# The input stage of a pool and RG-LRU decoder layer: order by a list scheduler in place of an order by hand

## The chip, the cores and the metric

The kernel runs on one core of a Trainium2 chip. The metric is device time in microseconds (us), the median of several executions; lower is better. The core has five engines that each work through their own list of instructions in order and meet at semaphores: TensorE (PE in the profile; its weight loads are PEld), VectorE (DVE), ScalarE (ACT), GpSimd (POOL) and SyncE (SP), which here issues every DMA.

## The reference

One layer of a decoder, in float32, over 2048 prompt tokens and 8 sequences of 8 new tokens (2112 tokens together, 1024 channels):

```
xn = rms_norm(x, norm_pre)
z  = xn @ w_in                                  # 1024 -> 4096: pool input V | gate G | lru input U | gate L
pool: causal means of V over windows 2/4/8/16 minus the token, one 256x256 map a group, a scale a channel
lru:  causal conv of width 4 on U -> r, i = sigmoid(block-diagonal maps)
      a = exp(-8 r softplus(-lam));  h = a h + sqrt(max(1 - a^2, 1e-12)) * i * u      # scan over time
out = concat(pool * silu(G), lru * silu(L)) @ w_out                                   # 2048 -> 1024
y   = x + rms_norm(out, norm_post)
```

The new states of the pool, the conv and the LRU are returned too.

## The kernel before, in words

Channels lie on the partitions and tokens along the free axis. Each float32 operand of a matrix product is split into a high and a low half of a reduced type (`split`, lines 123 to 131: a copy on ScalarE makes the high half, a subtraction makes the low one), and each product is three matmuls (high by high, high by low, low by high).

**Input stage.** The tokens are cut into three passes m of 704 (`MW`), each into two chunks of 352 columns. In a pass, the 32 blocks of 128 output channels are taken in 16 quads of two blocks: kind V, G, U or L, and p from 0 to 3. The list `QUADS` holds them in order. In pass 0 a quad is eight products of 12 matmuls (`plain_slot`). In passes 1 and 2 it is seven (a Strassen-like scheme, `quad_slot`, order 1, 5, 6, 3, 7, 2, 4 in `ORDER`); products 1, 6, 7 and 4 use one PSUM bank in turn (names a1V, a2G and so on in the profile), 5 and 3 a second (e), 2 a third (d). After each product the bank is emptied, by a copy on ScalarE (`put_copy`, L878) or a sum on VectorE (`put_sum`, L874), before the next product may use it. The seven combinations of x that the products multiply (X11, T1, T2, X22, T3, X21, T4) are made once for a pass, in the stretch called a transition, during the last quad of one pass and the first of the next. Those of the weights are made during passes 0 and 1, split, stored to DRAM (`wsd`), and loaded into half tiles (tag w, `W_BUFS` buffers of them) seven slots ahead of use (`w_step`).

Each finished quad starts a chain of work on the other engines: `silu_chain` for the gates, `pool_chain` (window sums, split, map, multiplication by the gate, store), and for the LRU `conv_chain`, then `lru_chain` (gates, exp, tanh, sqrt, a scan on VectorE, multiplication by the gate, store). `x_chain` prepares the tokens of the next pass. The chains keep their intermediate values in tiles of tag t (`T_BUFS`) and e (`E_BUFS`).

**What sets the order.** The stage is written under a manual schedule, so each engine runs its instructions as they are emitted. `one_slot` emits one product on TensorE, then the evacuations of the product before, then due DMAs, then pieces of chains. Each chain is a generator that yields what its next piece costs VectorE, ScalarE and GpSimd, in us, and how many slots to wait:

```
yield 0, 1.8, 0, 0        # lru_chain, after exp and tanh
return evac, {3: 0.5, 7: 0.5, 2: 0.5}.get(pid, 0.0)      # quad_slot: what an evacuation costs VectorE
```

`run_gens` goes on taking pieces while the slot's budget of 1.92 us (`SLOT`) an engine lasts. When a producer on another engine is done is not known to it; the number of slots to wait stands for that. What a transition emits in which slot is a table by hand (`plan` in `transition`). Stores go through `later`, which issues them two slots on.

**Output stage.** Eight pairs of token tiles, seven products each, with 512 columns a matmul. The first five first products (`p1`) are emitted inside the manual schedule, as 15 slots; the rest is ordered by the framework. Weights sit in regions 0, 1 and 2 of the old x storage; `combos_chain` makes the combinations of `w_out` during pass 2 and stores them (`wtd`), `region_chain` and `t3_chain` load and split them.

Of the kernel before, what the change touches and what calls it, by code (L numbers as in the profile page):

```python
# [55 lines left out]
SLOT = 1.92  # L56
# [7 lines left out]
def hymba_kernel(  # L64
# [656 lines left out]
    dmas, pe_q, gens = [], [], []  # L721
    now = [0]

    def later(slots, fn):
        dmas.append((now[0] + slots, fn))

    def due_dmas(force=False):
        for item in list(dmas):
            if force or item[0] <= now[0]:
                dmas.remove(item)  # L730
                item[1]()
# [3 lines left out]
    IDLE = [XN[:, BASE[n] + 1024 * i:BASE[n] + 1024 * (i + 1)] for n in ("X11", "T2", "T1") for i in range(2)]  # L735

# [7 lines left out]
    def store_w(flat, kind, p, pid, slots=2):  # L744
        key = (KINDS[kind] // 8 * NG + p) * 7 + pid - 1
        later(slots, lambda: nc.sync.dma_start(out=wsd[:, key, :], in_=flat.bitcast(F32)))

    def flat_of(t):
        return t.rearrange("p a b -> p (a b)")

    def plain_tile(q, n):
        t = w_tiles[q, n] = half_tile(f"w{q[2]}{q[1]}_{n}")
        split(t[:, 0, :], t[:, 1, :], w_rawt[q, n], AC, V)
        if n in PLAIN_PID:
            store_w(flat_of(t), q[2], q[1], PLAIN_PID[n])
        return 0.65, 0.62, 0.0

    n_idle = [0]

    def s_sums(q, i):  # L760
# [10 lines left out]
    S_OF = {5: "22", 6: "11", 7: "21", 3: "12"}  # L771

    def s_prep(q, i):
        if q[2] not in EARLY:
            return 0.0, 0.0, 0.0
        s_sums(q, i)
        dve, act = 0.65, 0.0
        for pid in ((), (5,), (6, 7), (3,))[i]:
            b = IDLE[n_idle[0] % len(IDLE)]
            n_idle[0] += 1  # L780
            split(b[:, :512], b[:, 512:], w_rawt[q, S_OF[pid]], AC, V)
            store_w(b, q[2], q[1], pid)
            dve, act = dve + 0.65, act + 0.62
        return dve, act, 0.0

    def w_step(q, i):
        m, p, kind = q
        pid = ORDER[i]
        t = w_tiles[q, pid] = half_tile(f"w{m}{kind}{p}_{pid}")
        if not is_late(q) or pid in (1, 2, 4):  # L790
            key = (KINDS[kind] // 8 * NG + p) * 7 + pid - 1
            nc.sync.dma_start(out=flat_of(t).bitcast(F32), in_=wsd[:, key, :])
        if not is_late(q) or i > 4:
            return 0.0, 0.0, 0.0
        if i < 4:
            s_sums(q, i)
        if not i:
            return 0.65, 0.0, 0.0
        split(t[:, 0, :], t[:, 1, :], w_rawt[q, S_OF[pid]], AC, V)
        store_w(flat_of(t), kind, p, pid)  # L800
        return 1.3 if i < 4 else 0.65, 0.62, 0.0
# [3 lines left out]
    def load_small(m, kind, p):  # L805
# [77 lines left out]
    def plain_slot(q, i):  # L883
        t = Q[q]
        j, h, c = PLAIN[i]
        n = f"{j + 1}{h + 1}"
        w = w_tiles[q, n]
# [5 lines left out]
        def evac():  # L893
            if h:
                put_copy(q, j, c, z)
            if i == 7:
                quad_end(q)
        return evac, 0.0

    def quad_slot(q, i):  # L900
# [3 lines left out]
        pid = ORDER[i]  # L904
        w = w_tiles.pop((q, pid))
# [4 lines left out]
        z = t[key]  # L910
        quad_product(z, w, XOF[pid], first, True, True)

        def evac():
            if pid == 1:
                put_copy(q, 0, 0, z)
            elif pid == 5:
                put_copy(q, 1, 1, z)
            elif pid == 6:
                put_copy(q, 0, 1, z)
            elif pid == 3:  # L920
                put_sum(q, 0, 1, z)
            elif pid == 7:
                put_sum(q, 1, 1, z)
            elif pid == 2:
                put_sum(q, 0, 0, z)
            else:
                put_copy(q, 1, 0, z)
                quad_end(q)
        return evac, {3: 0.5, 7: 0.5, 2: 0.5}.get(pid, 0.0)

    def spawn(gen, delay=1, need=0, rank=2):
        gens.append([gen, now[0] + delay, need, rank])
        gens.sort(key=lambda g: g[3])

    def quad_end(q):
        if q[2] in "GL":
            spawn(silu_chain(q), need=1)
        else:
            for g in {"V": lambda: [pool_chain(q)], "U": lambda: [conv_chain(q, j) for j in range(2)]}[q[2]]():
                spawn(g)  # L940

    def silu_chain(q):
        for j in range(2):
            g = Q[q]["dst"][j][:, :MW]
            AC.activation(out=g, in_=g, func=AF.Silu)
            yield 0, 0.85, 0, 0
# [7 lines left out]
    def pool_chain(q):  # L954
# [3 lines left out]
        c = L / 1000.0 * 1.05 + 0.1  # L958
        ds = []
        for j, blk in enumerate(blocks("V", p)):  # L960
            E = Q[q]["dst"][j]
            if m < LM:
                G.tensor_copy(out=hp[:, blk, :], in_=E[:, MW:MW + PB])
            else:
# [3 lines left out]
                later(3, lambda blk=blk, op=op: nc.sync.dma_start(out=o_pool[blk], in_=op))  # L968
            S, sh = E, 1
            while sh < w:  # L970
                while e_free() < 1:
                    yield 0, 0, 0, 1
# [5 lines left out]
                yield c, 0, 0.4 if sh == 1 else 0, 0  # L978
                S, sh = dst, 2 * sh
            if m == 0:  # L980
# [13 lines left out]
            yield c, 0, 0, 1  # L994
        Q[q]["d"] = []
        prev = Q.get((m, p - 1, "V") if p else (m - 1, NG - 1, "V"))
        while prev and not prev.get("maps"):
            yield 0, 0, 0, 1
        while t_free() < 1:
            yield 0, 0, 0, 1  # L1000
        load_small(m, "pw", p)
        for j, d in enumerate(ds):
            dh = e_tile(f"dh{m}_{p}{j}", F32R)[:, :MW]
            AC.copy(out=dh, in_=d)  # L1004
            yield 0, 0.8, 0, 1
            while e_free() < 1:
                yield 0, 0, 0, 1
# [4 lines left out]
            yield 0, 0, 1.8, 0  # L1012
        sums.add((m, p))
        yield 0, 0, 0, 3
        while not Q.get((m, p, "G"), {}).get("silu"):
            yield 0, 0, 0, 1
        for c in range(2):
            for j in range(2):
                pe_q.append((now[0] + 1, lambda j=j, c=c: pool_map(q, j, c)))

    def pool_map(q, j, c):
        m, p, _ = q
        pw = small["pw"]
# [6 lines left out]

# [3 lines left out]
        def evac():  # L1034
            assert Q[m, p, "G"].get("silu")
            V.scalar_tensor_tensor(out=g[:, cs], in0=Y, scalar=col(C_SCALE, blk), in1=g[:, cs],
                                   op0=ALU.mult, op1=ALU.mult)
            if c == 1:
# [3 lines left out]
                def store():  # L1042
                    nc.sync.dma_start(out=mixed[:, blk, m * MW:(m + 1) * MW], in_=g[:, :MW])
                    t_done(1)
                later(2, store)
        return evac, 0.55

    def conv_chain(q, j):
# [4 lines left out]
        while prev and not prev.get("gates"):  # L1053
            yield 0, 0, 0, 1
        while t_free() < (3 if j or m else 4):
            yield 0, 0, 0, 1
# [3 lines left out]
        E = Q[q]["dst"][j]  # L1060
        xs = t_chain(f"xs{b}_{m}")[:, :n]
# [8 lines left out]
        yield 0, 0.9, 0.4, 1  # L1070
        for k in range(CB):
            V.scalar_tensor_tensor(out=xs, in0=E[:, k:k + n], scalar=col(C_CW + 8 * k, b), in1=xs,  # L1072
                                   op0=ALU.mult, op1=ALU.add)
            yield 1.0, 0, 0, 0
# [3 lines left out]
        yield 0, 0.8, 0, 1  # L1078
        tsub(xl, xs, xh.bitcast(F32), G)
        yield 0, 0, 1.8, 2  # L1080
        rg = []
        for i in range(2):
            pe_q.append((now[0], lambda i=i: gate_mm(q, j, i, xs, xh, xl, rg)))

    def gate_mm(q, j, i, xs, xh, xl, rg):
        m, p, _ = q
        b = 2 * p + j
        lw = small["lw"]
# [640 lines left out]
```

## Time and profile before

| what | value |
|---|---|
| runs | 1299.25, 1294.89, 1299.58 us; median 1299.25 |
| the profiled execution | 1295.17 us, of which the span is 1293.5 |
| busy: PE, DVE, ACT, POOL | 1167.0, 901.0, 683.5, 327.6 us |
| mean granted TensorE clock | 0.954 |
| HBM traffic | 248 GB/s over the span |

The input stage proper runs from some 64 us to 930, its transitions at about 300 to 345 and 611 to 640; the p1 slots follow until 965, and the output stage to the end. A busy share is an average over stages, and a matmul's busy time is modelled. What counts for TensorE is how many matmuls a stretch holds and what the engine waited for at each gap; a row in a list of instructions has in brackets the idle time ahead of it and what ended it.

### The profile page before, as it was taken

What the parts mean: (1) busy time and instruction counts of PE and PEld (TensorE: products, weight loads), DVE (VectorE), ACT (ScalarE), POOL (GpSimd) and SP (SyncE); (2) the same over time, 40 slices, a digit from 0 to 9 for tenths busy, and PEclk for the clock granted to TensorE, in tenths of its full rate; (3) what the DMA queues carried; (4) which work ended last, traced back from release to release, by engine and by line L of the source; (5) the groups of instructions that cost most, each with busy time, mean ns of one, the idle gap of its engine ahead of it and who ended that gap; (6) DMA issues with size and microseconds to landing.
All of it is one profiled execution on the core that took longest, in us unless ns stands there. A gap on an engine that the chain in (4) does not pass through costs nothing. (4 is left out here: it accounts for less than half of the span.)

```text
span 1293.5 us, 17899 instructions
## 1 busy us (share of the span) xinstructions
PE 1167.0 (90%) x6274; PEld 1080.5 (84%) x6274; DVE 901.0 (70%) x1300; ACT 683.5 (53%) x1138; POOL 327.6 (25%) x340
## 2 busy tenths in 40 slices
PE   7999989998689897988889997899889999999987
PEld 6999989988689897987788897898867888888765
DVE  7887966878858766565845955567547668678667
ACT  5457578385496637374455823647744333234222
POOL 4232313133322131312323222424110002221322
PEclk9999989999799997998999998999998999999989
DMA  9367777855689784965777999888559966667553
GB/s 342 157 245 260 266 280 256 329 185 215 228 300 385 263 328 134 360 247 190 259 253 232 362 348 388 309 288 258 166 178 275 256 185 191 181 188 231 158 170 115
DMA packets 173306, 322.11 MB, mean 249 GB/s; under 512 B 17504, under 2 KB 79200, under 8 KB 173216
## 3 DMA queue, kind: packets, MB, share of 16 engines
q1 hardware_dynamic: 173216, 320.97, 72.6%
q8 instruction: 49, 0.80, 0.2%
q14 instruction: 41, 0.34, 0.1%
HBM read 218.51 MB, written 102.15 MB: 248 GB/s over the span
## 5 line engine op out<-in xcount | busy, mean ns | idle before, releaser
L441 PE MATMUL p<-XN,s 128*128 128x512 f32 (+1 forms) x224 | 88.8, 397 | 8.3 <-ACT s L128 8.3
L1072 DVE SCALAR_TENSOR_TENSOR xs<-u,parT,xs 128x704 f32<-128x704 f32 (+1 forms) x72 | 84.7, 1183 | 15.7 <-ACT xs L1062 12.7
L443 PE MATMUL p<-XN,s 128*128 128x512 f32 (+1 forms) x224 | 88.7, 396 | 2.6 <-DVE s L131 2.6
L1113 POOL TENSOR_TENSOR ig<-ig,xs 128x704 f32<-128x704 f32 (+1 forms) x24 | 45.1, 1879 | 175.6 <-ACT ig L1112 120.8
L442 PE MATMUL p<-XN,s 128*128 128x512 f32 (+1 forms) x224 | 88.2, 394 | 0.0
L306 POOL TENSOR_TENSOR xl<-xs,xh 128x704 fp32r<-128x704 f32 (+1 forms) x24 | 43.8, 1824 | 114.7 <-ACT xh L1077 112.9
L237 PE MATMUL zL<-XN,wL 128*128 128x352 f32 x384 | 64.9, 328 | 2.1 <-ACT wL L128 1.9
L237 PEld LDWEIGHTS zL<-XN,wL 128*128 128x128 f32 x384 | 63.2, 192 | 2.7 <-ACT wL L128 2.2
L128 ACT CAST s<-a 128x512 fp32r<-128x512 f32 x48 | 28.5, 618 | 65.5 <-DVE a L434 44.7
L237 PE MATMUL z<-XN,w 128*128 128x352 f32 x288 | 52.7, 343 | 7.6 <-ACT w L1324 5.4
L434 POOL TENSOR_TENSOR xr<-acw,xr 128x512 f32<-128x512 f32 x8 | 13.1, 1640 | 182.3 <-DVE acw L574 119.8
L441 PEld LDWEIGHTS p<-XN,s 128*128 128x128 f32 x224 | 43.3, 193 | 18.8 <-ACT s L128 9.1
L237 PEld LDWEIGHTS z<-XN,w 128*128 128x128 f32 x288 | 49.1, 199 | 10.6 <-ACT w L1324 5.4
L434 DVE TENSOR_TENSOR a<-a,a 128x512 f32<-128x512 f32 x48 | 34.0, 714 | 33.6 <-DMA a<-mixed 32.2
L306 POOL TENSOR_TENSOR dl<-s,dh 128x704 fp32r<-128x704 f32 x24 | 39.3, 1638 | 63.0 <-ACT dh L1004 42.7
L237 PE MATMUL zU<-XN,wU 128*128 128x352 f32 x288 | 50.6, 331 | 4.5 <-ACT wU L128 2.3
L237 PE MATMUL y<-dh,pw 128*128 128x352 f32 x192 | 54.6, 326 | 0.0
L442 PE MATMUL p<-XN,a 128*128 128x512 f32 x137 | 54.1, 395 | 0.0
L443 PE MATMUL p<-XN,a 128*128 128x512 f32 x137 | 54.1, 395 | 0.0
L441 PE MATMUL p<-XN,a 128*128 128x512 f32 x137 | 54.1, 395 | 0.0
L443 PEld LDWEIGHTS p<-XN,s 128*128 128x128 f32 x224 | 43.1, 192 | 13.1 <-DVE s L131 3.3
L434 POOL TENSOR_TENSOR xr<-ac,xr 128x512 f32<-128x512 f32 x19 | 33.2, 1761 | 80.9 <-issue 52.6
(350 smaller groups left out, 3432.9 us busy)
## 6 DMA issues: line engine op xcount, KB each, us to landing
a<-mixed SPq DMA_DIRECT2D x112, 256.0 KB, 4.0
mixed<-g SPq DMA_DIRECT2D x48, 352.0 KB, 6.2
w2V<-wsd SPq DMA_DIRECT2D x28, 512.0 KB, 5.4
w2G<-wsd SPq DMA_DIRECT2D x28, 512.0 KB, 5.1
w2U<-wsd SPq DMA_DIRECT2D x28, 512.0 KB, 5.5
w2L<-wsd SPq DMA_DIRECT2D x28, 512.0 KB, 6.5
wsd<-XN SPq DMA_DIRECT2D x24, 512.0 KB, 3.6
w1V<-wsd SPq DMA_DIRECT2D x24, 512.0 KB, 5.6
```

Source lines behind the costliest of these rows:

```text
L128: hi_eng.copy(out=hi, in_=src)
L237: nc.tensor.matmul(out, lhsT=lhsT, rhs=rhs, start=start, stop=stop)
L306: (eng or V).tensor_tensor(out=out, in0=a, in1=b, op=ALU.subtract)
L434: (eng or nc.vector).tensor_tensor(out=out, in0=a, in1=b, op=op)
L441: nc.tensor.matmul(out, lhsT=ah, rhs=wh, start=start and k == 0, stop=False)
L442: nc.tensor.matmul(out, lhsT=ah, rhs=wl, start=False, stop=False)
L443: nc.tensor.matmul(out, lhsT=al, rhs=wh, start=False, stop=stop and k == KT - 1)
L1072: V.scalar_tensor_tensor(out=xs, in0=E[:, k:k + n], scalar=col(C_CW + 8 * k, b), in1=xs, op0=ALU.mult, op1=ALU.add)
L1113: G.tensor_tensor(out=gi, in0=gi, in1=v, op=ALU.mult)
```

## The change

The slots' budgets are replaced by a list scheduler that runs while the program is built. It keeps a clock for VectorE, ScalarE and GpSimd (`clock`) and one for the slots (`T`). A chain becomes a job, whose generator yields requests: an engine and a duration, `"?"` and a condition, `"t"` and a time to pass, `"D"` (a DMA may be issued), `"P"` (a product for TensorE). A job's next request is ready 0.2 us (`HOP`) after the last one's end on its engine's clock. In each slot, evacuations come first; then, while one fits, the job that can start earliest is emitted. A request fits when it starts 0.2 us before the slot's end or earlier and ends at most 0.7 us (`OVER`) after it. ScalarE's table loads are counted, at 1.28 us. A slot ends after 1.94 us or when its evacuations do. Operands that a product needs at once are forced (`need_w`, `need_x`, `need_small`).

Beside that: half tiles go from 8 buffers to 6 and are loaded 6 slots ahead instead of 7; t tiles go from 14 to 17; the first G weights lie in x storage that is free at the time, and the first weight stores are issued earlier; the second half of the first L weights is split after product U in both chunks; the low halves of the small maps' weights are made on VectorE instead of GpSimd; `x_chain` for pass 1 starts a quad earlier; a region's weights are loaded one ahead; `combos_chain` starts when the first region is done; and the first seventh product of the output stage is loaded and prepared inside the p1 slots. In `lru_chain` the factor -0.25 and the maximum change places between two instructions, and the square root is emitted after the two VectorE steps that it stood between.

```
-SLOT = 1.92
+SLOT = 1.94
+HOP = 0.2
+OVER = 0.7
+AHEAD = 6
...
+    def takes(e, dur, fn=None):
+        if e == "A" and fn and table[0] not in TABLES[fn]:
+            return dur + 1.28
+        return dur
...
+    def fits(job, end):
+
+        e = job["req"][0]
+        if e in clock:
+            s = max(clock[e], job["ready"], T[0])
+            return s if s < end - 0.2 and (s <= T[0] + 0.1 or s + job["req"][1] < end + OVER) else None
+        return None
+
+    def run_jobs(end):
+        moved = True
+        while moved:
+            moved = False
+            for job in list(jobs):
+                while job in jobs:
+                    e, arg = job["req"][:2]
+                    if e == "?" and arg():
+                        job["ready"] = max(job["ready"], T[0])
+                    elif e == "t":
+                        job["ready"] += arg
+                    elif e == "D" and job["ready"] <= end:
+                        pass
+                    else:
+                        break
+                    advance(job)
+            best = None
+            for job in jobs:
+                s = fits(job, end)
+                if s is not None and (best is None or s < best[0] - 0.05):
+                    best = (s, job)
+            if best:
+                grant(best[1], best[0])
+                moved = True
...
-            split(t[:, 0, :], t[:, 1, :], r, AC, G)
+            yield "t", 4.0
+            yield "A", 0.62
+            AC.copy(out=t[:, 0, :], in_=r)
+            yield "V", 0.75
+            tsub(t[:, 1, :], r, t[:, 0, :].bitcast(F32))
             t_done(1)
-            later(2, lambda: nc.sync.dma_start(out=swd[:, i, p, :], in_=flat))
-        later(2, work)
+            yield "D", 0
+            nc.sync.dma_start(out=swd[:, i, p, :], in_=flat)
+        small[kind, "job"] = spawn(work(), rank=1)
...
-        return evac, {3: 0.5, 7: 0.5, 2: 0.5}.get(pid, 0.0)
+        return [("V", 0.52, evac) if add else ("A", 0.45, evac)]
...
+        yield "A", 1.96, "exp"
         AC.activation(out=v, in_=r, func=AF.Exp, scale=nlam[:, b:b + 1], bias=nlam[:, b:b + 1])
         AC.activation(out=r, in_=r, func=AF.Tanh, scale=lam2[:, b:b + 1], bias=lam2[:, b:b + 1])
-        yield 0, 1.8, 0, 0
+        yield "A", 0.87
         AC.activation(out=v, in_=v, func=AF.Identity, bias=ones[:, 0:1])
-        yield 0, 0.9, 0, 1
+        yield "V", 0.95
...
+        def put(n, eng="V"):
+            yield "?", lambda: slot_of[0] >= at[n]
+            yield "A", 1.37
+            x_hi(n, src[n])
+            yield eng, 3.4 if eng == "G" else 1.65
+            x_lo(n, src[n], {"V": V, "G": G}[eng])
+            done.add(n)
+            if n == "T4":
+                t_done(2)
...
+    def one_slot(pe_fn, prep_fn=None):
+
+        length = SLOT if pe_fn else 1.0
+        outs = pe_fn() if pe_fn else []
+        end = run_evacs(evacs)
+        evacs[:] = outs
+        for job in [j for j in jobs if j["req"][0] == "P"]:
+            if job["ready"] <= T[0] + 0.3:
+                evacs.extend(job["req"][1]())
+                length += 0.98
+                job["ready"] = T[0] + length + 0.5
+                advance(job)
+                break
+        if prep_fn:
+            prep_fn()
+        end = max(T[0] + length, end + 0.1)
+        run_jobs(end)
+        T[0] = end
+        n_slot[0] += 1
...
-            if (m == 0 and (qi, i) == (5, 0)) or (m == 1 and (qi, i) == (lasts[0] + 2, 4)):
-                spawn(x_chain(m + 1), 0, rank=0)
+            if (m == 0 and (qi, i) == (4, 0)) or (m == 1 and (qi, i) == (lasts[0] + 2, 4)):
+                spawn(x_chain(m + 1), rank=0)
             if m == 2 and (qi, i) == (lasts[1] + 2, 0):
-                spawn(region_chain(0, "b11", 0, 5), 0, rank=2)
-                spawn(combos_chain(), 20, rank=2)
+                spawn(region_chain(0, "b11", 0, 5), then=[lambda: spawn(combos_chain())])
...
+                        if g == 2:
+                            load_s3(0)
+                        if g == 4:
+                            prep_s3(0)
...
-    load_s3(0)
-    prep_s3(0)
...
-T_BUFS = 14
+T_BUFS = 17
...
-W_BUFS = 8
+W_BUFS = 6
```

More of the change, by code (lines that the diff above doesn't have):

```diff
@@ L720, in hymba_kernel @@
     w_tiles, w_rawt = {}, {}
[L721 to L731, printed above, removed]
+    jobs, pe_q, clock, T = [], [], {"V": 0.0, "A": 0.0, "G": 0.0}, [0.0]
+    table = ["sqrt"]
+    TABLES = {"silu": ("silu",), "exp": ("exp",), "sqrt": ("sqrt",), "tanh": ("silu", "exp")}
@@ new lines, in grant @@
+    def grant(job, start):
+        e, dur = job["req"][:2]
+        fn = job["req"][2] if len(job["req"]) > 2 else None
+        dur = takes(e, dur, fn)
+        if fn and table[0] not in TABLES[fn]:
+            table[0] = TABLES[fn][-1]
+        clock[e] = start + dur
+        job["ready"] = clock[e] + HOP
+        advance(job)
[5 more added lines that the diff above has]
+        return None
@@ L1052, in conv_chain @@
         prev = Q.get((m, p - 1, "U") if p else (m - 1, NG - 1, "U"))
[L1053 to L1056, printed above, removed]
+        yield "?", lambda: (not prev or prev.get("gates")) and t_free() >= (3 if j or m else 4)
         t_live[0] += 3
```

493 lines of the change are left out of this document (259 added, 234 removed).

## The prediction, written before the result was known

> **What bounds the kernel now.** I read the page first, then busy time by stage, then what TensorE waited for, then each engine's rows around the longest waits.
>
> ```profile
> span 1293.5 us, 17899 instructions
> ```
>
> ```profile
> PE 1167.0 (90%) x6274; PEld 1080.5 (84%) x6274; DVE 901.0 (70%) x1300; ACT 683.5 (53%) x1138; POOL 327.6 (25%) x340
> ```
>
> TensorE is busy longest. By stage (columns: length, busy time and count of PE, PEld, DVE, ACT, POOL, then granted clock, DMA share, GB/s):
>
> ```profile
> 50.00:75.00 25.00, 25.00 (x158) 25.00 (x157) 20.40 (x27) 14.38 (x19) 2.52 (x2) 1.00 0.39 137
> 64.00:300.00 236.00, 225.01 (x1349) 220.82 (x1348) 182.22 (x223) 158.06 (x259) 70.56 (x65) 0.97 0.70 254
> 300.00:372.00 72.00, 52.49 (x299) 50.76 (x297) 56.38 (x64) 38.52 (x59) 20.57 (x12) 0.88 0.76 270
> 372.00:674.00 302.00, 268.12 (x1550) 261.29 (x1550) 194.98 (x245) 174.99 (x267) 77.08 (x82) 0.94 0.76 269
> 674.00:750.00 76.00, 67.25 (x385) 66.18 (x386) 55.57 (x72) 50.27 (x74) 23.92 (x31) 0.93 0.82 296
> 750.00:930.00 180.00, 161.80 (x955) 158.82 (x953) 105.91 (x145) 92.84 (x144) 53.77 (x74) 0.95 0.84 296
> ```
>
> The first row has no gap: 25/158 = 0.158 us a matmul, so a slot of 12 is 1.90 us. The other five (the input stage that the change orders, 866 us) hold 4538 matmuls, 718 us at that rate. So **148 us are lost**: 91 us of idle TensorE (866 less the five busy times), and 57 us of matmuls at a lower clock, for which the clocks of 0.88 to 0.97 stand. The longest waits of TensorE (total, times, longest):
>
> ```profile
> PE a1V L235 <- ACT e L878: 12.5, 2, 12.1
> PE a2U L235 <- ACT u L878: 9.3, 3, 5.3
> PE a1L L235 <- ACT g L878: 8.5, 5, 2.7
> ...
> PE a2V L235 <- DVE e L874: 8.0, 1, 8.0
> ```
>
> L878 and L874 are the copy and the sum that empty a PSUM bank, so TensorE waits for small evacuations on ScalarE and VectorE, not for its weights. Product 1 must be copied out before product 6 adds to the same bank, with only product 5 between: one slot of slack. One such wait (ScalarE, then TensorE):
>
> ```profile
> 504.43 0.44 ACT L878 COPY g<-e1L 128x352 f32<-128x352 f32 x1
> 504.89 1.28 ACT L1115 ACT_TABLE_LOAD   x1
> 506.18 0.98 ACT L1115 ACTIVATE xs<-rg,nlam 128x704 f32<-128x704 f32 x1
> 507.19 0.97 ACT L1116 ACTIVATE rg<-rg,lam 128x704 f32<-128x704 f32 x1
> 508.07 0.86 ACT L1118 ACTIVATE xs<-xs,ones 128x704 f32<-128x704 f32 x1
> 508.84 0.60 ACT L128 CAST w1U<-wr1U 128x512 fp32r<-128x512 f32 x1
> 509.35 0.44 ACT L878 COPY g<-a1L 128x352 f32<-128x352 f32 x1
> ```
>
> ```profile
> 509.84 1.54 PE L235 MATMUL a1L<-XN,w1L 128*128 128x352 f32 x4 [2.74 <-ACT g L878]
> ```
>
> ScalarE never stops: 4.5 us of work stand between two copies. The hand's budget counts the copy (0.0) and the exp table load not at all. The other kind, in the first transition (ScalarE, VectorE, GpSimd, TensorE):
>
> ```profile
> 330.65 0.78 ACT L319 CAST XN<-rt 128x704 fp32r<-128x704 f32 x1 [2.98 <-DVE rt L306]
> ...
> 333.56 0.45 ACT L878 COPY e<-a1V 128x352 f32<-128x352 f32 x1
> ```
>
> ```profile
> 326.72 3.85 DVE L306 TENSOR_TENSOR rt<-XA,rt 128x704 f32<-128x704 f32 x1
> 330.49 0.88 DVE L306 TENSOR_TENSOR XN<-dg,XN 128x704 fp32r<-128x704 f32 x1
> ```
>
> ```profile
> 325.95 3.86 POOL L306 TENSOR_TENSOR XN<-XA,XN 128x1408 fp32r<-128x1408 f32 x1 [8.99 <-ACT XN L321]
> ```
>
> ```profile
> 334.06 2.42 PE L235 MATMUL a1V<-XN,w1V 128*128 128x352 f32 x7 [12.12 <-ACT e L878]
> ```
>
> Here ScalarE stands idle in front of a cast whose input is late, and the copy that TensorE needs is queued behind it. VectorE's subtraction is itself late: 3.85 us beside a GpSimd operation of 3.86, 0.88 us just after.
>
> **The change part by part.** The arithmetic stays: every pass has as many operations as before, the LRU chain too, where only scale and maximum trade places. What changes is order, prefetch and buffers.
>
> *Evacuations.* The new planner puts them first in a slot, with 0.45, 0.52 or 0.58 us each, counts table loads, and starts a piece of a chain only when its producer's clock has passed and the piece ends at most 0.7 us after the slot. For the exp case: copy 0.44, load 1.28, two activations 0.98 + 0.97, next copy 0.44: 4.11 us from the slot's start, due after two slots, 3.80. The gap goes from 2.74 to 0.31: 89% less. That is the upper bound for gaps of this kind. As the lower one I take 50%, since durations scatter (0.88 to 3.85 above) and a fixed order can't answer that. Without the two largest gaps (12.1 and 8.0) the idle time is 71 us; at 70%, midway, **50 us** come back (36 to 63).
>
> The Trainium skill (ScalarE: Activation LUTs, What ACT_TABLE_LOAD costs) prices a switch of tables at about 2.66 us, a drain of 1.38 being added to the load. By that the exp case would take 5.49 us and leave a gap of 1.69, and the 50 would be nearer 27. In the rows the activation starts 0.01 us after the load's end and the load 0.02 after the copy, so I see no drain and keep 1.28.
>
> *Transition.* The copy no longer stands behind the cast, so of the 12.1 us about 3 (3.85 less 0.88) can stay: **9 us** back (0 to 12). But the stage from 300 to 372 has 56.4 us of VectorE work for 299 matmuls, 47.3 us: VectorE bounds it, and unless work moves out of it **9 us** of its loss stay (0 to 9). The first X preparation starts a quad earlier, which hides in the stage before (VectorE 182 of 236 us); without that cover it would cost its eight row scalings inside the transition, which these 9 us stand for.
>
> *The 8.0 us gap* is a VectorE evacuation behind `combos_chain`:
>
> ```profile
> DVE wo L306 <- DMA wo<-in_w_out: 25.3, 6, 8.8
> ```
>
> ```profile
> 775.00:800.00 25.00, 17.01 (x89) 16.93 (x89) 11.62 (x17) 5.54 (x10) 5.57 (x10) 0.80 0.99 367
> ```
>
> The DMA engines are full there. The new chain reads the next rows one step ahead and waits 5.0 us between steps, much as before: **0** back (-8 to 8).
>
> *Clock.* The 57 us of slow matmuls follow the gaps, so they shrink in the same share: (50 + 9)/91 of 57 = **37 us** (22 to 52).
>
> *Seam.* The first seventh-product operand is now loaded and prepared inside the p1 slots, and its weights (region 1) are loaded one ahead:
>
> ```profile
> 972.55 0.79 PE L441 MATMUL p<-XN,s 128*128 128x512 f32 x1 [7.03 <-ACT s L128]
> 973.14 0.63 PE L442 MATMUL p<-XN,s 128*128 128x512 f32 x1
> ```
>
> The gap goes, and the slow matmuls after it: **8 us** (0 to 9). What is late next is the region's own splits, on the same two engines.
>
> *Weight tiles.* 8 buffers and a lead of 7 slots become 6 and 6. Tile n+6 now reuses the buffer of product n, so its load, issued by SP in order and behind whatever store stands there, can start only when product n ends and has 5 slots, 9.5 us; before it was 7 slots, 13.3 us. To landing it takes:
>
> ```profile
> w2V<-wsd SPq DMA_DIRECT2D x28, 512.0 KB, 5.4
> ...
> w1G<-wsd SPq DMA_DIRECT2D x24, 512.0 KB, 7.8
> ```
>
> ```profile
> DMA to landing us min/median/max: 2.6/7.7/14.3
> ```
>
> (The last row is w1G alone, between 300 and 600 us.) The medians land in time; the worst would be 4.8 us late. The passes 1 and 2 use 224 tiles: with one in a hundred that late, 2 × 4.8, it costs **10 us**, with four in a hundred 40 (0 to 40). I take the value near the medians. Stores are now issued as soon as their producer's modelled clock has passed, instead of two slots later; a late GpSimd result then holds SP, and these tiles are what waits behind. That is in the 40.
>
> *At nothing or little.* The low halves of the eight small matrices move from GpSimd to VectorE. Their price there is that of the same shape:
>
> ```profile
> 281.18 2.39 POOL L131 TENSOR_TENSOR pw<-pwr,pw 128x512 fp32r<-128x512 f32 x1 [15.39 <-DMA wr0L<-in_w_in]
> ```
>
> ```profile
> L131 DVE TENSOR_TENSOR s<-a,s 128x512 fp32r<-128x512 f32 x48 | 32.5, 695 | 3.2 <-ACT s L128 3.1
> ```
>
> 8 × 0.7 = 5.6 us, hidden in VectorE's idle 54 us of the first pass, else 5.6. Two plain weight tiles of the first quad now wait until product U has released their buffers and hold VectorE's scalings behind them: **2 us** (0 to 4), two casts and subtractions of 0.6 and 0.7 each. The first stores go to SP earlier, ahead of the first quad's raw loads; I cost that at nothing, since TensorE has no gap from 50 to 75 us (first stage row), else one store's few us. Fourteen chain buffers become 17, which only lets chains run longer.
>
> *New gaps.* A planner that fills engines has less room for error. VectorE's 182 us in the first pass must fit 213 us of matmuls, 85%. No row shows a plan that doesn't exist; bounds are 0 and two thirds of today's idle, 60. I take **20**, a third of that, because the conv's price in the plan, 1.2, is the measured mean with its disturbances:
>
> ```profile
> L1072 DVE SCALAR_TENSOR_TENSOR xs<-u,parT,xs 128x704 f32<-128x704 f32 x48 | 58.4, 1221 | 10.1 <-ACT xs L1062 7.6 <-POOL g L1147 1.9
> ```
>
> Sum: 50 + 9 + 37 + 8 = 104 back, 9 + 10 + 2 + 20 = 41 paid, 63 net. The profiled execution took 1295.2 us (span 1293.5 and 1.7 around it), so **1232 us**. The median of the runs shown is 1299.25, 0.3% above that execution.
>
> **The rivals.** (a) *A small gain*: VectorE drifts behind the plan, because GpSimd holds it up as at 326.72, and the planner's clocks hold no such term. GpSimd's 246 us in the five stages say how often that can be; that the mean conv is priced with it speaks against. New gaps cost 60 instead of 20: 1272 us. The Trainium skill (SBUF — State Buffer, Who interferes with whom) has this as a rule: a VectorE instruction with two SBUF inputs and a reading GpSimd instruction shut each other out for a whole instruction. By it the trace's pair agrees.
>
> (b) *Slower*: weight loads become the bound in passes 1 and 2. At full rate the last two stages' 256 us become 212, and their 296 GB/s 357, close to the 367 of the full window. If tiles come late by 0.25 us in the mean, 224 × 0.25 = 56 us, with clock loss (148/91) 91 instead of 10: 1313 us. It decides from about 0.2 us a tile. Against it: no wait of TensorE names a DMA today, and the heavy window is short.
>
> (c) *It doesn't do what it says*: the engines run ahead of the plan's 1.94 us slots or behind them, waits just move, and the idle share stays: 1295 us.
>
> **How the numbers follow.** Forecast (1195 to 1265): 0.60. Better than 1195: 0.03. (a), 1265 to 1292: 0.17. (c): 0.07. (b): 0.13. About 0.5% is what a measurement here can tell from no change. Faster 0.80, same 0.07, slower 0.13. The range 1195 to 1298 leaves out 0.03 below and most of (b) above.
>
> **What would show it.** Idle TensorE time between the same stages of about 50 us, with ScalarE's copies no more than one large operation behind a bank's last matmul; clocks of 0.97 or more; the 12.1 and 7.0 us gaps gone; the 8.0 us gap still there. Waits of TensorE for a DMA into w1 or w2 would show (b); subtractions of several us on VectorE beside GpSimd ahead of evacuations, (a). The prediction is wrong if evacuations still make up some 80 us.

## The result and the profile after

The median goes from 1299.25 to **1236.52 us** (runs 1239.46, 1236.52 and 1233.32). The ratio of the runs to those of the kernel before is 0.953, 95% interval 0.948 to 0.958. The profiled execution of the kernel after took 1239.46 us, that of before 1295.17. Its first lines:

```profile
span 1237.6 us, 17847 instructions
PE 1147.4 (93%) x6274; PEld 1064.7 (86%) x6274; DVE 905.7 (73%) x1308; ACT 680.5 (55%) x1138; POOL 347.1 (28%) x332
```

The amount of work is the same. To see where the 56 us of span come from, both traces are cut at the same places of the work and not at the same times: pass 0 from its first product, transition 1 (first product of pass 1, a1V, to the first of its second quad, a1G), the rest of pass 1, transition 2, the rest of pass 2, the p1 slots with the seam, and the output stage. The busy times by stretch of the kernel before, cut in this way (columns as in the prediction: length, then busy time and count of PE, PEld, DVE, ACT and POOL, then granted clock, DMA share and GB/s):

```profile
63.69:313.03 249.34, 238.35 (x1432) 234.16 (x1431) 194.08 (x237) 165.20 (x267) 72.35 (x66) 0.97 0.71 257
313.03:345.78 32.75, 17.52 (x86) 16.71 (x86) 27.25 (x30) 13.21 (x21) 10.08 (x6) 0.74 0.62 212
345.78:632.98 287.20, 251.38 (x1443) 243.91 (x1443) 191.25 (x238) 173.15 (x262) 73.13 (x72) 0.94 0.76 276
632.98:650.29 17.31, 17.31 (x110) 17.31 (x109) 13.09 (x15) 6.71 (x13) 8.61 (x8) 1.00 0.71 220
650.29:930.94 280.65, 250.41 (x1473) 246.08 (x1471) 170.65 (x230) 157.66 (x239) 82.46 (x112) 0.95 0.83 294
930.94:972.55 41.61, 31.55 (x126) 25.07 (x127) 22.73 (x34) 22.43 (x35) 6.94 (x8) 0.89 0.59 175
972.55:1293.50 320.95, 306.03 (x1312) 246.10 (x1312) 233.48 (x420) 112.54 (x237) 53.01 (x30) 0.97 0.66 194
```

The same view of the kernel after:

```profile
64.23:312.27 248.04, 234.75 (x1433) 232.51 (x1431) 175.38 (x237) 159.91 (x261) 59.13 (x53) 0.97 0.72 263
312.27:332.42 20.15, 15.76 (x87) 14.93 (x85) 17.73 (x22) 14.58 (x19) 8.20 (x7) 0.92 0.67 232
332.42:592.68 260.26, 245.18 (x1456) 240.27 (x1456) 193.60 (x239) 157.02 (x244) 76.17 (x66) 0.96 0.88 308
592.68:613.49 20.81, 15.06 (x85) 14.22 (x85) 19.31 (x19) 14.07 (x20) 12.06 (x9) 0.95 0.61 190
613.49:874.33 260.84, 244.09 (x1466) 239.80 (x1465) 187.24 (x241) 164.82 (x247) 104.44 (x119) 0.98 0.91 322
874.33:907.44 33.11, 31.99 (x145) 26.32 (x144) 23.27 (x29) 29.24 (x43) 8.03 (x6) 1.00 0.64 183
907.44:1237.60 330.16, 306.30 (x1312) 245.84 (x1312) 241.85 (x428) 111.59 (x241) 58.36 (x34) 0.97 0.66 193
```

| stretch | before, us | after, us | difference |
|---|---|---|---|
| start, to the first product | 63.7 | 64.2 | +0.5 |
| pass 0 | 249.3 | 248.0 | -1.3 |
| transition 1 | 32.8 | 20.2 | -12.6 |
| pass 1 | 287.2 | 260.3 | -26.9 |
| transition 2 | 17.3 | 20.8 | +3.5 |
| pass 2 | 280.7 | 260.8 | -19.8 |
| p1 slots and seam | 41.6 | 33.1 | -8.5 |
| output stage | 321.0 | 330.2 | +9.2 |

Three things are to be seen. First, the input stage's five stretches, 867.3 us, become 810.1. TensorE's busy time in them (first number after the length, summed) falls from 775.0 to 754.8, and its idle time, length less busy, from 92.3 to 55.3. So of the 57 us, 37 are waits that went and 20 are the same matmuls run faster. Second, nearly all of it comes from passes 1 and 2 and the first transition; pass 0 hardly gains. Third, the output stage, which the change hardly touches, is 9 us longer at the same TensorE work (306.0 and 306.3): that is idle time.

What TensorE waits for in the kernel after (total, times, longest), the first eight rows:

```profile
PE r L240 <- ACT xh L1161: 8.2, 1, 8.2
PE a1U L238 <- ACT u L976: 6.8, 2, 3.9
PE p L444 <- ACT s L131: 6.6, 2, 5.5
PE z L240 <- ACT w L1438: 5.5, 1, 5.5
PE p L446 <- DVE s L134: 5.5, 6, 2.7
PE a2V L238 <- DMA w2V<-wsd: 4.8, 1, 4.8
PE a1G L238 <- ACT g L976: 3.8, 2, 3.0
PE a2V L238 <- issue: 3.7, 1, 3.7
```

L976 and L972 are the evacuations now, L878 and L874 were. Summed over all rows of this list that name them, TensorE waited 79.4 us for evacuations before and 25.3 after; all its waits together went from 116.6 to 80.9. The new first row is no evacuation: it is the gate product, whose input is late. The sixth is a half tile's load.

**The worked case of the prediction.** ScalarE with the exp in the kernel after:

```profile
475.53 0.98 ACT L1201 ACTIVATE xs<-rg,nlam 128x704 f32<-128x704 f32 x1
476.54 0.98 ACT L1202 ACTIVATE rg<-rg,lam 128x704 f32<-128x704 f32 x1
477.43 0.43 ACT L976 COPY g<-a1G 128x352 f32<-128x352 f32 x1
477.75 0.88 ACT L1204 ACTIVATE xs<-xs,ones 128x704 f32<-128x704 f32 x1
478.54 0.87 ACT L1220 ACTIVATE w<-w,epsT 128x704 f32<-128x704 f32 x1
479.32 0.43 ACT L976 COPY g<-a1L 128x352 f32<-128x352 f32 x1
479.76 1.28 ACT L1034 ACT_TABLE_LOAD   x1
481.06 0.79 ACT L1034 ACTIVATE g<-g 128x704 f32<-128x704 f32 x1
481.76 0.43 ACT L976 COPY g<-e1L 128x352 f32<-128x352 f32 x1
```

Between two copies stand two operations or a table load and one, where four and a table load stood before. Copies follow each other by 1.9 and 2.4 us, near the slot's 1.94, and TensorE's waits behind the last two are 0.48 us (until 479.80) and 0.26 us (until 482.24), where one of 2.74 us stood before. The table load's 1.28 us end at 481.04, and the next operation starts at 481.06, with no drain between.

**Why pass 0 hardly gains.** It has a new stall of 8.2 us. ScalarE, then TensorE, then SyncE's queue ahead of them, then busy times by stretch:

```profile
192.50 0.62 ACT L911 CAST pw<-pwr 128x512 fp32r<-128x512 f32 x1 [12.86 <-DMA pwr<-in_pool_w]
193.03 0.77 ACT L1161 CAST xh<-xs 128x704 fp32r<-128x704 f32 x1
```

```profile
193.86 0.66 PE L240 MATMUL r<-xh,lw 128*128 128x352 f32 x1 [8.20 <-ACT xh L1161]
```

```profile
176.15 7.26 SPq L338 DMA_DIRECT2D wr0U<-in_w_in  x4
...
185.67 0.33 SPq L903 DMA_DIRECT2D pwr<-in_pool_w  x1
```

```profile
180.00:185.00 5.00, 5.00 (x35) 5.00 (x34) 0.00 (x0) 0.00 (x0) 0.45 (x1) 1.00 1.03 415
185.00:190.00 5.00, 0.65 (x5) 0.36 (x3) 0.00 (x0) 0.00 (x0) 0.00 (x0) 0.84 0.98 384
```

The cast of a small map's weights stands on ScalarE waiting for its DMA for 12.9 us. The gate's cast xh stands behind it with its input ready, the gate's product waits for xh, and in order after it the whole of TensorE. The DMA was issued only at 185.67, behind four loads that held SyncE for 7.26 us and one store. SyncE's waits in these 7.26 us are for earlier DMAs (4.9 us, the longest, 3.1 us, for a load of XA, the x of pass 1, which the change loads a quad earlier), and the DMA engines are full at 384 to 415 GB/s. The planner's clocks know three engines; the DMA is a fixed 4.0 us in the job (`yield "t", 4.0`).

### The profile page after: what moved, and what is told of

Same layout as the page of the kernel before. It is cut to its first block, busy times and chain, and to the rows that moved or that the text cites. A ratio compares the mean times of both kernels' runs of the same rounds, so it can differ in the third digit from the quotient of the medians.

```text
span 1237.6 us, 17847 instructions
## 1 busy us (share of the span) xinstructions
PE 1147.4 (93%) x6274; PEld 1064.7 (86%) x6274; DVE 905.7 (73%) x1308; ACT 680.5 (55%) x1138; POOL 347.1 (28%) x332
## 5 line engine op out<-in xcount | busy, mean ns | idle before, releaser
L437 POOL TENSOR_TENSOR xr<-ac,xr 128x512 f32<-128x512 f32 x27 | 49.5, 1854 | 239.4 <-issue 124.3
L1156 DVE SCALAR_TENSOR_TENSOR xs<-u,parT,xs 128x704 f32<-128x704 f32 (+1 forms) x72 | 91.3, 1280 | 1.9 <-ACT xs L1145 1.5
L557 ACT ACTIVATE p<-ac 128x512 f32<-128x512 f32 (+1 forms) x32 | 18.8, 588 | 99.2 <-DVE ac L437 98.7
L1120 DVE SCALAR_TENSOR_TENSOR g<-y,parT,g 128x352 f32<-128x352 f32 x48 | 27.9, 581 | 56.9 <-PE y L240 56.9
L309 POOL TENSOR_TENSOR xl<-xs,xh 128x704 fp32r<-128x704 f32 (+1 forms) x24 | 48.7, 2030 | 70.1 <-ACT xh L1161 67.4
L444 PEld LDWEIGHTS p<-XN,s 128*128 128x128 f32 x224 | 43.3, 193 | 16.9 <-ACT s L131 7.7
L446 PEld LDWEIGHTS p<-XN,s 128*128 128x128 f32 x224 | 43.0, 192 | 16.9 <-DVE s L134 7.3
L445 PEld LDWEIGHTS p<-XN,s 128*128 128x128 f32 x224 | 43.1, 192 | 11.3 <-DVE XN L309 1.2
L240 PE MATMUL zG<-XN,wG 128*128 128x352 f32 x288 | 48.8, 330 | 2.7 <-ACT wG L822 2.3
```

Of the source, the lines that this page charges most:

```text
L240: nc.tensor.matmul(out, lhsT=lhsT, rhs=rhs, start=start, stop=stop)
L309: (eng or V).tensor_tensor(out=out, in0=a, in1=b, op=ALU.subtract)
L437: (eng or nc.vector).tensor_tensor(out=out, in0=a, in1=b, op=op)
L444: nc.tensor.matmul(out, lhsT=ah, rhs=wh, start=start and k == 0, stop=False)
L445: nc.tensor.matmul(out, lhsT=ah, rhs=wl, start=False, stop=False)
L446: nc.tensor.matmul(out, lhsT=al, rhs=wh, start=False, stop=stop and k == KT - 1)
```

## The experiments

My theory: the gain comes from the planner knowing when a producer on another engine is done (readiness), and from the true prices of ScalarE's copies and table loads only after that; what is left is lost to inputs that come by DMA. The rivals: the prices alone are worth most of it; the smaller lead of the half tiles costs much; VectorE bounds the transitions. Ratios compare the runs with those of the kernel before on the same chip (medians 1291.1 to 1295.6 us), with 95% intervals.

**Without prices.** ScalarE's copies and table loads cost the planner nothing; all else stays.

```
-        if e == "A" and fn and table[0] not in TABLES[fn]:
-            return dur + 1.28
...
-            clock[e] = max(clock[e], T[0]) + dur
+            clock[e] = max(clock[e], T[0]) + (0.0 if e == "A" else dur)
```

> The changed kernel, whose planner now prices ScalarE as the hand did: copies out of PSUM at nothing and no table loads. Theory (the gain is mostly that a copy no longer stands behind more ScalarE work than a slot holds): TensorE idle time in the five input stages rises from 55 us by 15 to 35, ScalarE is busy ahead of the gaps, time 1255 to 1290 us. Rival (the gain comes from waiting for producers, the prices matter little): within 6 us of the changed kernel, 1230 to 1243.

Measured: 1260.9 us, 0.974 (0.971 to 0.977). Waits for evacuations are 29.3 us against 25.3. The idle time of the five stretches is 72.5 us against 55.3, which the theory had at 70 to 90; 6.1 of the 17 more are one wait for the first operand of the p1 slots. More than half of the gain stays without these prices. The difference is some 2% of the time. But other prices bring another order, and orders alone differ by 1 to 2.5% here (below), so that this is what the prices are worth isn't shown.

**Readiness 2 us early.** A producer counts as done 2.0 us before its end on the planner's clock. The prices stay.

```
-HOP = 0.2
+HOP = -2.0
```

> The changed kernel with HOP at -2.0 instead of 0.2: a piece may be emitted 2 us before its producer's end in the plan, all prices kept. Theory (readiness is the other half of the gain): ScalarE and VectorE stand idle in front of late inputs with evacuations queued behind, as before the change; idle TensorE time in the input stages up by 10 to 30 us, time 1250 to 1280 us. Rival (prices alone do it, each engine catches up): within 6 us, 1230 to 1243.

Measured: 1319.6 us, 1.019 (1.014 to 1.023): slower than the change by 6.6% of the time before, some 86 us, and slower than the kernel before. The sign was as expected, the size was not. TensorE's first waits:

```profile
PE r L240 <- DMA lw<-swd: 27.7, 5, 7.0
PE y L240 <- DMA pw<-swd: 19.4, 5, 7.3
PE y L240 <- ACT pw L911: 16.1, 2, 10.9
```

Evacuations are 28.2 us, hardly more than in the change. What is lost is lost on TensorE's own list: r and y are the products of the gates and the maps, which the planner also places. Placed too early they wait for a DMA or a cast, and all products behind them wait too. So what an early plan costs here, it costs where the planner places work on the engine that bounds.

Neither run brings the waits for evacuations back (29.3 and 28.2 us, 79.4 before), though they are what the change took away. Either the prices or the readiness alone is enough for them, or they went by something that both runs keep: smaller pieces, the limit at the slot's end, buffers, earlier loads. No run separates these.

**The prices in the order by hand.** The kernel before, with true costs in its budgets: the copy 0.45, exp with its table load 3.2, silu 1.5.

```
-            yield 0, 0.85, 0, 0
+            yield 0, 1.5, 0, 0
...
-        yield 0, 1.8, 0, 0
+        yield 0, 3.2, 0, 0
...
+        bud[1] -= 0.45 * len(outs)
```

> The kernel before, its order by hand, with ScalarE's true prices in its budgets: 0.45 us a copy out of PSUM, exp with its table load 3.2 instead of 1.8, a silu with its share of a load 1.5 instead of 0.85. Theory (the prices were half of what was wrong with it): less ScalarE work stands ahead of the copies, 1260 to 1285 us by the scale of 1295 for the kernel before. Rival (without knowing when a producer is done, prices move work later and make chains longer): within 1% of the kernel before, or slower.

Measured: 1312.6 us, 1.015 (1.011 to 1.019): slower. TensorE's first wait:

```profile
PE a1V L235 <- ACT e L878: 27.0, 2, 15.5
```

The copy behind a transition's casts, 12.5 us before, now waits 27.0. My reading, which no run tests: chains that get less of each slot run later into the transition, whose table by hand doesn't know it. Waits for evacuations stay at 81.0 us. That the prices alone bring most of the gain, put into the order by hand, falls.

**Half tiles.** First the buffers and the lead as before, for which t tiles must go down to 15; beside it t tiles at 15 alone.

```
-AHEAD = 6
+AHEAD = 7
...
-T_BUFS = 17
+T_BUFS = 15
...
-W_BUFS = 6
+W_BUFS = 7
```

> Seven weight half tiles and a lead of 7 slots, paid for with 15 chain tiles instead of 17. Theory (the shorter lead costs what the waits of TensorE on w2 loads show, 7.5 us of idle time, and clock): those waits go, 5 to 12 us less than the run with 15 chain tiles and 6 half tiles. Rival (the loads are late because SP stands at another tile, so a slot more of lead doesn't help): no more than 3 us apart.

> The changed kernel with 15 chain tiles instead of 17, half tiles and lead kept at 6. If 17 chain tiles carry part of the gain, it is slower by 5 to 20 us, chains being held back at the quads' starts; if they only let chains run longer, within 4 us.

Measured: 1276.9 us, 0.985 (0.982 to 0.988), against 1243.9, 0.961 (0.957 to 0.964) with t tiles at 15 alone. The latter is 0.8% above the change, within what a new order does. I expected the longer lead to give 5 to 12 us and it cost 33. The comparison was a bad one: a product's lead decides when its split is spawned as a job, so the whole plan came out in another order. It says nothing on the lead.

So the same with the lead left at 6, where the input stage's instructions keep the order that they have at T 15 alone, and the buffer is only free a slot earlier:

```
-T_BUFS = 17
+T_BUFS = 15
...
-W_BUFS = 6
+W_BUFS = 7
```

> The run with 15 chain tiles, with 7 half tiles instead of 6 and the lead left at 6 slots: the input stage's order is the same, and a load no longer waits for the product that held its buffer last. Theory (the buffers' wait is what makes weight loads late): the waits of TensorE on w1 and w2 loads, 14 us in the run with 6, fall to 5 or less, 8 to 15 us less. Rival (loads are late by the DMA engines' load and SP's other waits): within 4 us.

Measured: 1242.8 us, 0.964 (0.961 to 0.967), the same as T 15 alone. TensorE's waits for loads of half tiles go from 17.8 to 11.1 us, and the five stretches of the input stage from 830.8 to 823.0 us; the output stage, in an order of its own, goes from 316.8 to 325.7 and takes it back.

**The load in front of a half tile.** In the kernel after, TensorE's longest wait for a half tile has this on SyncE:

```profile
730.69 6.83 SPq L940 DMA_DIRECT2D sp<-in_st_pool  x2
737.61 0.38 SPq L870 DMA_DIRECT2D w2V<-wsd  x1
```

SyncE stands 5.5 us for the one buffer of sp, and the tile's load behind it. A second buffer takes the wait away; each engine's order stays as it is.

```
-tag="sp", bufs=1
+tag="sp", bufs=2
```

> The changed kernel with two buffers instead of one for the small tile that takes the pool states in pass 2; every engine's order stays as it was. Theory (the waits of TensorE on w2V at 734 to 742 us, 4.8 and 0.9, come from SP standing for 6.8 us at the second load of that tile, the weight loads being queued behind): those waits go, 6 to 9 us less with clock, pass 2 from 261 us to some 253. Rival (five slots are too short for a full DMA, whatever SP does): the waits stay, less than 3 us.

Measured: 1228.6 us, 0.951 (0.948 to 0.955). The 4.8 us wait is gone, all waits for half tiles fall from 7.5 to 5.2 us, and pass 2 takes 258.4 us for 260.8 (253 was expected). A gain isn't measured: the interval lies inside that of the change. In this trace a VectorE evacuation is 2.0 us later (4.4 for 2.4), and others move by less.

**The stall of pass 0.** The planner is told 12 us for the small maps' loads.

```
-            yield "t", 4.0
+            yield "t", 12.0
```

> The changed kernel with 12 us instead of 4 in the plan between the load of a small map's weights and their split. Theory (the gaps of 8.2 and 1.8 us at 186 to 196 us come from ScalarE standing 12.9 us in front of that split, the load being late): they go, pass 0 from 248 us to 237 or so, 8 to 13 us less. Rival (the plan is greedy, moving one piece moves everything after it, and as much is lost elsewhere): pass 0 shorter, but the whole within 6 us or slower.

Measured: 1226.9 us, 0.952 (0.949 to 0.955), no different from the change. The 8.2 us stall goes, and pass 0 falls from 248.0 to 241.4 us. Pass 1 grows from 260.3 to 270.1; one row of TensorE's waits is

```profile
PE r L240 <- DMA lw<-swd: 6.9, 1, 6.9
```

the same mechanism one load further on. The gain in one place was real; the plan behind it came out otherwise.

**How much any edit shuffles.** A slot of 1.95 us for one of 1.94, which should do nothing.

```
-SLOT = 1.94
+SLOT = 1.95
```

> The changed kernel with slots of 1.95 us instead of 1.94 in the plan, a change of no meaning for the chip. Theory (the plan fits, small changes of its prices change little): within 4 us. Rival (a greedy order is chaotic: it shuffles and the time shows by how much): 5 to 20 us off, in either direction.

Measured: 1243.0 us, 0.965 (0.961 to 0.968). On the same chip the order of the change, with two sp buffers, has 0.951 (0.948 to 0.955). So this edit costs 1.3%, with intervals that don't meet: pass 1 takes 278.6 us for 260.3, with

```profile
PE r L240 <- ACT xh L1161: 22.6, 3, 10.0
```

A greedy plan turns any small change of its numbers into another order. Orders differ by 1.3% here, and by 2.5% between the two runs with 15 t tiles whose lead differs. A single edit that reorders can't be judged below that.

**The transitions.** The low halves of X22 and X21 go from GpSimd to VectorE.

```
-            x_jobs["X22"] = spawn(put("X22", "G"), T[0], rank=0)
+            x_jobs["X22"] = spawn(put("X22", "V"), T[0], rank=0)
```

(X21 likewise.)

> The changed kernel with the low halves of X22 and X21 made on VectorE instead of GpSimd. If GpSimd's four long subtractions hold VectorE up in the transitions for more than they save it, the two transitions (20 and 21 us) get shorter by 2 to 6 us together and no VectorE subtraction of 4 us is left in them; if VectorE bounds the transitions, they get longer by 3 to 6 us. The whole: within 10 us, the order of what follows being shuffled.

Measured: 1249.6 us, 0.967 (0.964 to 0.969), slower than the change, but not in the transitions. These stretches in the kernel of the experiment:

```profile
311.04:328.44 17.40, 14.87 (x85) 13.41 (x85) 16.39 (x20) 13.92 (x18) 0.72 (x1) 1.00 0.83 284
...
608.95:624.31 15.36, 14.26 (x87) 13.36 (x85) 14.65 (x19) 8.49 (x13) 4.68 (x5) 1.00 0.62 225
```

They take 32.8 us for 41.0 together, and none of VectorE's subtractions in them is stretched any more. VectorE's busy time in them falls from 37.0 to 31.0 us, but that says less, since the shorter stretches also hold fewer of its instructions, 33 for 41. In the kernel after, VectorE's two subtractions just ahead of transition 1 stand beside a GpSimd one:

```profile
309.65 4.74 DVE L309 TENSOR_TENSOR XA<-XA 128x704 f32<-128x704 f32 x2
309.87 3.76 POOL L309 TENSOR_TENSOR XN<-XA,XN 128x1408 fp32r<-128x1408 f32 x1 [5.42 <-ACT XN L324]
```

0.88 us each is their time alone, so 3 us were lost, and TensorE's wait for the low half, 3.3 us, follows. So GpSimd beside VectorE holds these transitions up. How much of the 8.2 us is due to it isn't shown: the kernel with slots of 1.95 us, whose low halves stay on GpSimd, has transitions of 17.2 and 17.2 us, 6.5 less than the change by another order alone. The 20 us that pass 1 has more (280.5) are a reordering like that of the slot's length: here GpSimd holds other work than before, and TensorE waits 42.0 us for evacuations.

**The seam.** The first seventh product's loading and preparation go back behind the p1 slots.

```
-                        if g == 2:
-                            load_s3(0)
-                        if g == 4:
-                            prep_s3(0)
...
+    load_s3(0)
+    prep_s3(0)
```

> The changed kernel with the first seventh product's operand loaded and prepared behind the p1 slots again; the input stage's order is the same. Theory (this part gave the 8 us of the seam): a gap of about 7 us on ScalarE's split is back at the start of the output stage, 5 to 9 us slower. Rival (the region's splits, now loaded one ahead, were the brake): within 3 us.

Measured: 1235.0 us, 0.955 (0.953 to 0.957). The stretches of the seam and of the output stage in this kernel:

```profile
870.81:909.89 39.08, 31.99 (x145) 26.32 (x145) 27.27 (x34) 31.36 (x47) 10.47 (x10) 0.95 0.60 173
909.89:1231.30 321.41, 304.06 (x1312) 245.99 (x1312) 237.04 (x422) 112.28 (x238) 54.90 (x30) 0.97 0.67 196
```

The gap of before is back (7.1 us), and the seam takes 39.1 us for 33.1. But the output stage takes 321.4 for 330.2, as it did before the change. Over the whole kernel the part made no difference that these runs show. The framework orders the output stage anew in each build, and its length depends on what was taken out ahead of it.

**More margin.** A producer counts as done 0.6 us after its end on the planner's clock instead of 0.2, with two sp buffers.

```
-HOP = 0.2
+HOP = 0.6
```

> Two buffers for the pool states' tile, and 0.6 us instead of 0.2 between a producer's end and its consumer's start in the plan. If late inputs at the head of a queue are what is left (a plan 2 us early cost some 85), a margin helps: 5 to 20 us less than the changed kernel. If the order is only shuffled: 1% either way; if chains get too long: slower.

Measured: **1219.1 us, 0.943** (0.940 to 0.945). It beats both kernels, and on the same chip the kernel with the seam put back (0.955). Its passes 0 and 2 in the busy times by stretch:

```profile
65.55:298.00 232.45, 230.08 (x1432) 228.33 (x1431) 187.39 (x246) 171.59 (x273) 65.81 (x57) 1.00 0.77 284
...
602.94:850.67 247.73, 236.61 (x1453) 232.71 (x1452) 181.01 (x229) 156.49 (x236) 92.47 (x114) 1.00 0.92 336
```

Both run at the full clock; pass 0 has 2.4 us of idle TensorE left (13.3 in the change) and pass 2 11.1 (16.8). With 1 to 2.5% from a reshuffle, this kernel doesn't tell whether the margin or the order that it happened to bring is the cause. The two ends of the scale (-2.0 and 0.6) do fit one picture.

## Why the prediction was right, and where it wasn't

The forecast was 1232, from a profiled execution of 1295.2: 63 us net. The profiled executions differ by 55.7 us, the medians by 62.7. The place of the gain was the one described: TensorE's waits for evacuations. The terms were further off than the total. The total came this near in part by luck, since errors cancel: 19 us more back from idle time than the sum had, 17 less from the clock, and 10 paid that it didn't have. By kind:

| kind | by the sum, us | measured, us |
|---|---|---|
| idle time in the five stretches: 50 + 9 back, 41 paid | 18 back | 37 back |
| their matmuls at a faster clock | 37 back | 20 back |
| seam | 8 back | 8.5 back |
| output stage and start | 0 | 9.7 paid |

By its own steps:

- **Evacuations, 50 (36 to 63), and the two largest gaps, 9 + 0.** Together 59 were expected. Measured 54 (79.4 less 25.3): both large gaps gone, 12.1 and 8.0, and 34 of the other 59. So small evacuation waits shrank by 57% and not by 70%, and the base of 71 us held some 12 us that were no evacuations; the 8.0 us gap made up for it. Which part of the change did it stays open. The exp case went about as priced (0.48 us left, 0.31 said). The Trainium skill (ScalarE: Activation LUTs, What ACT_TABLE_LOAD costs) has 2.66 us for a switch with its drain; here it is 1.28 plus 0.02, and the 27 that followed from it would have been too few.
- **The 8.0 us gap, "still there": wrong.** The chain now starts when the first region is done, and its loads run from 654.8 to 768.1 us. The DMA engines are full there too (379 to 390 GB/s from 665 to 715 us and from 740 to 765), and a load lands no faster (median 6.7 us, 6.4 before). VectorE's wait for them still fell from 25.3 us to this, and no run shows why:

```profile
DVE wo L309 <- DMA wo<-in_w_out: 8.1, 3, 4.2
```

- **Transition, VectorE-bound, 9 paid: wrong in its reason.** Transition 1 gained 12.6 us. The 56.4 us of VectorE work that the prediction counted there held stretched operations like its own row of 3.85 us for 0.88, which it took into the term only for 3 us of one gap. In the kernel after, the largest wait in each transition follows such rows: 3.3 us in the first (above), and 3.7 us in the second, which the profile puts down to nothing ("issue"). It ends at 610.64, 0.1 us behind VectorE's sum out of that bank. Ahead of the sum VectorE has three operations of 3.93, 1.90 and 2.36 us, each beside a GpSimd one; alone they take 0.94, 0.88 and 0.88. The rule of the Trainium skill (SBUF — State Buffer, Who interferes with whom), that a VectorE instruction with two SBUF inputs contends with a GpSimd one that reads SBUF, agrees with these rows.
- **Clock, 37 (22 to 52).** The faster matmuls give 20 us: the mechanism was right, the size too large. The term was scaled by the 59 us that go, without the new gaps that come; with the 37 of 92 that went net, the prediction's own proportion gives 23. Transitions and pass 1 still have clocks of 0.92 to 0.96, where 0.97 or more had been said, because waits of some 3 us are left there (last section).
- **Seam, 8 (0 to 9).** 8.5 us in that stretch. The whole kernel doesn't show it, since the output stage moves the other way. The output stage had no term in the sum, and it cost 9.2: the largest one missed.
- **Weight tiles, -10 (0 to 40).** TensorE waits 7.5 us for half tiles, the longest (4.8) behind a load that holds SyncE, as the term said of stores. One more buffer for them takes some 7 us of such waits away without moving the total.
- **New gaps, -20.** Idle time other than for evacuations rose from 12.9 to 30.0 us (92.3 less 79.4, 55.3 less 25.3). So 17 were paid where the sum had set 41 aside for all causes. The gaps are there, but of another kind: not VectorE drifting from its plan but mostly 8.2 + 1.8 us in front of the gate's product for a small map's DMA, and single waits of 2 to 5 us. By the rows above, the 3.3 and 3.7 us in the transitions are of the kind named: VectorE held up by GpSimd.
- **Rivals.** (a), GpSimd holding VectorE, is true in the transitions; the two waits above are 7 us, and moving the low halves gave 8 at most, not 40. (b), loads as the bound, isn't so in this plan. (c) doesn't hold: idle time in the five stretches fell from 92 to 55 us. The 50 named as the sign of the forecast was near; the sum itself, with all that it paid, would have left over 70.

**What stays open.** Why the framework's order of the output stage is 9 us longer in the change (317 to 330 us among the builds here). What took the waits for evacuations away, prices, readiness or the rest of the change. Why pass 2 of the kernel with a lead of 7 is 20 us longer than that with T 15 alone. Whether a margin of 0.6 is better in general, or only in this order.

## What to carry to other kernels

Where engines run in the order written, a planner with clocks can pay: 4.7% here. A plan that was 2 us early lost that and more, and true prices did not help the order by hand. Give the planner every resource that can be late (here DMA issue and landing were a constant, and the largest new stall was one of them), and try a margin, above all for what it places on the engine that bounds. Since a greedy plan moves by 1 to 2.5% with any of its numbers, try several and keep the best, and judge a single edit in the stretch that it touches, with the order otherwise unchanged.

## What the runs showed of the hardware

- The clock falls after waits of some 2 us, not after short ones. In the five stretches of the kernel after, TensorE has 15 waits of 0.5 to 1.5 us, and the 2 us behind each show a granted clock of 1.00; of its 11 waits of 1.8 to 8.2 us, 10 are followed by a lower one, down to 0.50. In pass 1 (0.96 in the mean) windows of 2 us show it low in three stretches only, of 8 to 10 us each, at the waits of 2.96, 3.91 and 2.88 us. Behind the prediction's gap of 2.74 us a product of 12 matmuls takes 3.89 us, where 2.08 is usual.
- Full DMA engines went with a held issuer: four loads held SyncE for 7.26 us, 4.9 of them waiting for earlier DMAs, while 415 GB/s moved, and a 256 KB load behind them landed 6.8 us after its own issue.
- A table switch cost the load's 1.28 us and 0.02 beside it in the rows of the exp case.
